# First layer's MLP gate moved from VectorE to TensorE, and the second layer's modulation issued piece by piece, in a two-layer hybrid diffusion backbone

## The chip, the cores and the metric

The kernel runs on one core of a Trainium2 chip. The metric is the device time of one execution in microseconds; the time before is the median of three runs, 2549.3 us (2545.8 to 2554.59). PE below is TensorE, DVE is VectorE, ACT is ScalarE, POOL is GpSimd, and SP is the engine whose queue issues nearly all loads and stores.

## The reference, cut to what matters

Two layers run over 512 latent and 256 context tokens of 1024 features. Each layer makes six vectors of modulation for each of the two streams from a conditioning vector, and uses them as shift, scale and gate around the attention (the first three) and around the MLP (the last three).

```python
mod   = silu(c) @ w_mod[l] + b_mod[l]          # 6 * 1024 values, latent stream
mod_c = silu(c_ctx) @ w_mod[l] + b_mod[l]      # the same, context stream
sh1, sc1, g1, sh2, sc2, g2 = split(mod, 6)     # kinds 0, 1, 2, 3, 4, 5 below
h = modulate(rms_norm(x), sh1, sc1)
...                                            # projections, three attention branches, merge
x = x + g1 * y
x = x + g2 * square(relu(modulate(rms_norm(x), sh2, sc2) @ w_mlp_in)) @ w_mlp_out
```

The second layer updates the latent stream alone. "Kind 5" below is g2, the gate of the MLP.

## The kernel before

The residual is kept transposed: features on the 128 partitions (8 tiles `x[j]`), tokens on the free axis, 768 in the first layer and 512 in the second. Every float32 product is made of three products of rounded parts and remainders (`wh`, `wl` of a weight, `hh`, `hl` of an activation). A weight arrives in pieces of 128x1024 (512 KB): SP loads `wr` (two buffers), ACT rounds it to `wh`, POOL makes the remainder `wl` (`piece`, L197 and L199).

A layer runs as phase 1 (projections; chunk by chunk of 256 columns, products `pb` at L481 to L483, then norms and rotations on DVE, results stored to DRAM), phase 2 (attention with the gate logits `g` between its steps), phase 3 (merge and output projection) and phase 4 (MLP). The MLP runs over eight groups g of 512 hidden features: `up(g + 1)` makes the next group's squared relu (PSUM tile `mi`, `r` and `uh` on ACT, `u` on POOL, `ul` on DVE at L1307) and `down(g)` adds group g into the residual (PSUM tile `mo`; on DVE `x += g2 * mo` at L1261, called resid below, once for 512 and once for 256 tokens of each of 8 feature tiles).

The modulation is made in three ways. (1) `mod_first` makes kinds 0 and 1 of the first layer on PE. (2) `mod_units` makes kinds 2, 4 and 3 of the first layer on PE during its projections: 24 pieces of 128x1024 (tile `wm`, two buffers, loaded by SP at L306), four pieces for a unit of 512 features; after every chunk of the projections two pieces are multiplied (`mod_pe`, L266: 8 small products a piece, 32 columns wide, four of them in the four column groups of the array); after the fourth piece ACT copies the sum out, PE transposes it (L274), and two small DVE steps write `mod` (L314). (3) `mod_step` makes the rest on DVE in the first layer's MLP: one step loads a piece (`wm<-in_wmod`, L249, again two buffers of the name `wm`) and multiplies and sums it over the free axis (L252, called a reduction below), once for each stream that is asked for. 56 steps are queued by `mod_start`: kind 5 of the first layer and kinds 1 and 0 of the second for both streams (24 steps, 48 reductions), and the other four kinds of the second for the latent stream (32 steps, 32 reductions). They are issued eight ahead of `down(0)` and nine after each `down`.

The program is written in the order of these functions; a scheduler then sets the order of each engine's queue from priorities and its own estimate of when things are ready. An engine runs its queue strictly in order, SP too.

Of the kernel before, what the change touches and what calls it, by code (L numbers as in the profile page):

```python
"""Two layers of the hybrid diffusion backbone (MLA + windowed GQA + differential attention).

The residual stream is kept transposed (features on partitions, tokens on the free axis, latent
tokens first, context tokens after them).  Products run in float32r: every float32 operand is split
exactly into a rounded part and a remainder, and the three products that matter at float32
accuracy (hi*hi, lo*hi, hi*lo) are accumulated in PSUM.
"""
# [27 lines left out]
# columns of w_in  # L35
C_QLAT, C_KVLAT, C_KPE, C_SQ, C_SK, C_SV, C_DQ, C_DK, C_DV, C_G = (
    0, 256, 384, 416, 928, 1056, 1184, 1696, 2208, 2720)
# rope order of a head: [first halves of row and column | second halves of row and column]
# [3 lines left out]
# broadcast vectors of a layer  # L42
V_MQ, V_MK, V_SQ, V_SK, V_DQ, V_DK, V_SINK, V_L = 0, 96, 192, 256, 320, 384, 448, 456
NV = 456 + 256
# per-partition vectors of a layer
P_GA, P_GM, P_BM, P_GQ, P_GKV, P_GS = 0, 8, 16, 64, 66, 67
NP_ = 68
# constants
# [30 lines left out]
def _layout(inp):  # L79
    """Host side: permutations and concatenations only."""  # L80
    g = {n: np.asarray(a) for n, a in inp.items()}
    f = lambda a: np.ascontiguousarray(a, dtype=np.float32)
    o = {}
# [3 lines left out]
    # units of four feature blocks: shift and scale of the first norm by pairs of feature tiles, then kinds 2, 4 and 3  # L87
    a = g["w_mod"][0, :, :2048].reshape(KT, 128, 2, 4, 256).transpose(3, 1, 0, 2, 4)
    o["wm0"] = f(a.reshape(4, 128, KT * 512))
    a = g["w_mod"][0].reshape(4, 2, 128, 6, 2, 512)[:, :, :, [2, 4, 3]].transpose(3, 4, 0, 2, 1, 5)  # L90
    o["wm1"] = f(a.reshape(6, 4, 128, 1024))
# [45 lines left out]
class Build:  # L137
    def __init__(self, tc, ins, out):
        self.tc = tc
        self.nc = tc.nc  # L140
        self.ins = ins
        self.out = out
        self.n = 0
        self.mq = []
        self.early = False
        self.gains = {}
        self.F1, self.WD, self.WC = 0.3, 1.5, 0.4   # how the gates are spread over the attention
        self.px = 0

# [11 lines left out]
    def R(self, name, dt=F32):  # L161
        """a [128, 768] tile of the phase's pool"""
# [8 lines left out]
    def psx(self, name):  # L171
        """one bank for a dense product, from both tags in turn"""
# [16 lines left out]
    def piece(self, src, n=1024, own=0):  # L189
        """hi, lo of a piece of weights; own: the number of slots it takes of the phase's pool in place of the common  # L190
        ones."""
# [10 lines left out]
    def mm3(self, out, ah, al, bh, bl, start, stop):  # L202
        """out += (ah + al).T @ (bh + bl) but for al.T @ bl."""
# [9 lines left out]
    def dense_steps(self, ps, w, x, c):  # L213
        """ps = sum of w.T @ x[:, c]; w: [(hi, lo)] stationary [128, 128] blocks, x: [(hi, lo)] moving."""
# [8 lines left out]
    def split_sb(self, src, n=768):  # L223
        """hi, lo of an SBUF tile."""
# [7 lines left out]
    def mod_start(self, kinds):  # L232
        """queue up mod = silu(c) @ w_mod + b_mod for the given sixths, features on partitions."""
# [27 lines left out]
    def mod_pe(self, w, ks, ps):  # L261
        """ps[32 g + stream, 128 features] += 2 silu(c) @ w for four feature blocks g; w [128, len(ks), 512]."""
# [7 lines left out]
    def mod_out(self, ps, pt):  # L270
        """[128 features, 4 blocks, 32]: twice the modulation without its bias."""
# [5 lines left out]
    def mod_first(self, q):  # L277
        """shift and scale of the first norm for feature tiles 2q and 2q + 1, in two steps."""
# [18 lines left out]
    def mod_units(self, n):  # L297
        """n pieces of the modulation of kinds 2, 4 and 3 of the first layer."""
        nc = self.nc
        for _ in range(n):  # L300
            if self.mu == 24:
                return
# [7 lines left out]
            if i == 3:  # L310
                v = self.mod_out(self.mps, self.mps[:, 512:640])
                o = (2, 4, 3)[u // 2] * 8 + u % 2 * 4
# [4 lines left out]
    def first_norm(self, x, h):  # L317
        """the first norm, feature tiles as their modulation arrives, and the query latent of the first layer: PSUM
        tiles [128 tokens, 256]."""
# [45 lines left out]
    def norm_gain(self, l, which, s, k=None):  # L365
        """128 * g * (1 + scale) per feature (rows_rsq gives 1 / 128); of feature tiles k and k + 1 alone at every even k."""
# [19 lines left out]
    def add_square(self, acc, x, j, c, sq, eng):  # L386
        """acc += x_j ** 2 on columns c; sq: a scratch tile."""
# [1142 lines left out]
```

## Time and profile before

| what | value |
|---|---|
| median of three runs | 2549.3 us |
| lowest and highest run | 2545.8, 2554.59 us |
| span of the profiled execution (first to last instruction) | 2547.0 us |
| PE busy, share of the span | 2432.5 us, 96% |
| DVE busy, share of the span | 1537.6 us, 60% |
| first layer's projections | about 84 to 270 us |
| first layer's MLP | about 935 to 1490 us |

The page gives no other time of that execution than its span, which is 2.3 us below the median of the runs. PE is the busy engine throughout; the time that it stands idle is 114.5 us (2547.0 less 2432.5). In the tables of waits, a row names the engine that waited, the tile that it was to write and its line, and behind the arrow what it waited for; then the sum in us, how often, and the longest.

### The profile page before, as it was taken

The numbers are of one execution on the slowest core, as the hardware profiler recorded it, in microseconds if no ns is written. First come the engines' busy times: TensorE is split into PE (matmuls) and PEld (weight loads), VectorE is DVE, ScalarE is ACT, GpSimd is POOL, SyncE is SP. The second block draws the span as 40 slices with busy tenths as digits, with TensorE's granted clock in tenths as the row PEclk, the third lists the DMA queues.
The fourth block names the chain that finished last, engine by engine and source line by source line (L and its number), as shares of the span: only waits on it lengthen the run. The fifth ranks groups of instructions, "written<-read, shape, count | busy, mean of one in ns | idle before, by whom it ended". The sixth has DMA issues, their size and how long they took to land. (4 is left out here: it accounts for less than half of the span.)

```text
span 2547.0 us, 40061 instructions
## 1 busy us (share of the span) xinstructions
PE 2432.5 (96%) x15466; PEld 2136.6 (84%) x15466; DVE 1537.6 (60%) x3081; ACT 1079.7 (42%) x2105; POOL 915.1 (36%) x629
## 2 busy tenths in 40 slices
PE   6999999999999998999999989999999999999999
PEld 5989888888888887888888989998878777888888
DVE  6547777878874479872222277777788874621112
ACT  4343566667652233212222244346666632422321
POOL 2434211111115326434333354441222235454543
PEclk9999999999999999999999999999999999999999
DMA  7265322222346225662111122443323344222222
GB/s 280 90 222 203 131 97 84 96 77 94 100 137 226 94 76 171 214 231 75 59 67 66 60 99 86 173 153 95 103 83 118 110 156 155 83 92 99 91 100 83
DMA packets 133182, 307.38 MB, mean 121 GB/s; under 512 B 43264, under 2 KB 49536, under 8 KB 132608
## 3 DMA queue, kind: packets, MB, share of 16 engines
q1 hardware_dynamic: 122624, 281.23, 32.6%
q10 hardware_dynamic: 10368, 23.60, 2.4%
q8 instruction: 122, 2.00, 0.3%
q14 instruction: 68, 0.56, 0.1%
HBM read 252.08 MB, written 52.70 MB: 120 GB/s over the span
## 5 line engine op out<-in xcount | busy, mean ns | idle before, releaser
L199 POOL TENSOR_TENSOR wl<-wr,wh 128x1024 fp32r<-128x1024 f32 (+2 forms) x266 | 652.6, 2457 | 1139.2 <-ACT wh L197 1066.8
L197 ACT ACTIVATE wh<-wr 128x1024 fp32r<-128x1024 f32 (+2 forms) x266 | 279.5, 1052 | 581.2 <-PE mo L219 317.6
L218 PE MATMUL mo<-uh,wh 128*128 128x512 f32 (+1 forms) x832 | 286.4, 344 | 18.6 <-DVE x L1261 13.6
L219 PE MATMUL mi<-hl,wh 128*128 128x512 f32 (+1 forms) x832 | 285.7, 344 | 3.3 <-DVE hl L434 3.3
L220 PE MATMUL mi<-hh,wl 128*128 128x512 f32 (+1 forms) x832 | 285.2, 343 | 0.0
L218 PE MATMUL mi<-hh,wh 128*128 128x512 f32 (+1 forms) x832 | 284.8, 344 | 0.3 <-DVE x L1261 0.3
L219 PE MATMUL mo<-ul,wh 128*128 128x512 f32 (+1 forms) x832 | 283.8, 341 | 0.0
L220 PE MATMUL mo<-uh,wl 128*128 128x512 f32 (+1 forms) x832 | 283.1, 341 | 0.0
L1307 DVE TENSOR_TENSOR ul<-u,uh 128x512 fp32r<-128x512 f32 (+1 forms) x104 | 80.7, 777 | 304.0 <-POOL u L1306 301.7
L1261 DVE SCALAR_TENSOR_TENSOR x<-mo,mod,x 128x512 f32<-128x512 f32 (+1 forms) x208 | 127.9, 625 | 200.6 <-PE mo L220 200.6
L481 PE MATMUL pb<-wh,hh 128*128 128x256 f32 (+1 forms) x832 | 244.2, 294 | 0.0
L482 PE MATMUL pb<-wl,hh 128*128 128x256 f32 (+1 forms) x832 | 243.2, 292 | 0.8 <-POOL wl L199 0.8
L483 PE MATMUL pb<-wh,hl 128*128 128x256 f32 (+1 forms) x832 | 243.3, 293 | 0.0
L218 PE MATMUL g<-hh,wh 128*128 128x512 f32 (+1 forms) x576 | 212.2, 368 | 0.0
L220 PE MATMUL g<-hh,wl 128*128 128x512 f32 (+1 forms) x576 | 211.8, 368 | 0.0
L219 PE MATMUL g<-hl,wh 128*128 128x512 f32 (+1 forms) x576 | 211.5, 367 | 0.0
L868 ACT ACTIVATE pth<-pT 128x512 fp32r<-128x512 f32 (+3 forms) x344 | 154.1, 462 | 101.7 <-PE pT L865 90.4
L218 PEld LDWEIGHTS mo<-uh,wh 128*128 128x128 f32 x832 | 157.3, 189 | 39.1 <-DVE x L1261 14.9
L869 DVE TENSOR_TENSOR ptl<-pT,pth 128x512 fp32r<-128x512 f32 (+3 forms) x344 | 171.9, 516 | 24.8 <-ACT pth L868 22.6
L219 PEld LDWEIGHTS mi<-hl,wh 128*128 128x128 f32 x832 | 157.3, 189 | 23.5 <-DVE hl L434 3.7
L218 PEld LDWEIGHTS mi<-hh,wh 128*128 128x128 f32 x832 | 156.8, 189 | 20.4 <-DVE x L1261 0.5
L220 PEld LDWEIGHTS mi<-hh,wl 128*128 128x128 f32 x832 | 157.3, 189 | 19.8
(243 smaller groups left out, 5932.5 us busy)
## 6 DMA issues: line engine op xcount, KB each, us to landing
wr<-in_wmi SPq DMA_DIRECT2D x64, 512.0 KB, 3.5
wr<-in_wmo SPq DMA_DIRECT2D x64, 512.0 KB, 3.5
wm<-in_wmod SPq DMA_DIRECT2D x56, 512.0 KB, 3.6
wr<-in_wg SPq DMA_DIRECT2D x48, 512.0 KB, 3.6
wr<-in_wb SPq DMA_DIRECT2D x36, 512.0 KB, 4.2
wm<-in_wm SPq DMA_DIRECT2D x28, 512.0 KB, 4.5
wr<-in_wup SPq DMA_DIRECT2D x24, 512.0 KB, 3.5
gd<-gt ACTq DMA_DIRECT2D x24, 384.0 KB, 2.4
```

What stands on the lines that cost most here:

```text
L197: nc.scalar.activation(out=hi[:, :n], in_=raw[:, :n], func=AF.Copy)
L199: nc.gpsimd.tensor_tensor(out=lo[:, :n], in0=raw[:, :n], in1=hi[:, :n].bitcast(F32), op=ALU.subtract)
L218: mm(ps, lhsT=wh, rhs=xh[:, c], start=i == 0, stop=False)
L219: mm(ps, lhsT=wh, rhs=xl[:, c], start=False, stop=False)
L220: mm(ps, lhsT=wl, rhs=xh[:, c], start=False, stop=i == n - 1)
L481: mm(ps[:, :n], lhsT=ah[:, cs], rhs=wh, start=k == 0, stop=False)
L482: mm(ps[:, :n], lhsT=ah[:, cs], rhs=wl, start=False, stop=False)
L483: mm(ps[:, :n], lhsT=al[:, cs], rhs=wh, start=False, stop=k == nk - 1)
L868: nc.scalar.activation(out=hv[:, k0:k0 + n, qs], in_=pv, func=AF.Copy)
L869: nc.vector.tensor_tensor(out=lv[:, k0:k0 + n, qs], in0=pv, in1=hv[:, k0:k0 + n, qs].bitcast(F32), op=ALU.subtract)
L1261: self.nc.vector.scalar_tensor_tensor(out=x[j][:, c], in0=ps, scalar=g, in1=x[j][:, c], op0=ALU.mult, op1=ALU.add)
L1307: nc.vector.tensor_tensor(out=b[:, c], in0=u, in1=a[:, c].bitcast(F32), op=ALU.subtract)
```

## The change

Kind 5 of the first layer becomes two more units of `mod_units`: 32 pieces in place of 24, three after each of the first four chunks of the projections and two after each of the ten others. `mod_start` no longer queues it, so 48 steps are left (16 for both streams, 32 for the latent one, 64 reductions). They are issued two at a time ahead of each weight piece of `down`, eight per group. The comments go as well, so line numbers above 1300 differ by a few; below that they stay.

```diff
-    a = g["w_mod"][0].reshape(4, 2, 128, 6, 2, 512)[:, :, :, [2, 4, 3]].transpose(3, 4, 0, 2, 1, 5)
-    o["wm1"] = f(a.reshape(6, 4, 128, 1024))
+    a = g["w_mod"][0].reshape(4, 2, 128, 6, 2, 512)[:, :, :, [2, 4, 3, 5]].transpose(3, 4, 0, 2, 1, 5)
+    o["wm1"] = f(a.reshape(8, 4, 128, 1024))
...
     def mod_units(self, n):
         for _ in range(n):
-            if self.mu == 24:
+            if self.mu == 32:
                 return
...
-                o = (2, 4, 3)[u // 2] * 8 + u % 2 * 4
+                o = (2, 4, 3, 5)[u // 2] * 8 + u % 2 * 4
...
             F[f]()
             if l == 0:
-                self.mod_units(2)
+                self.mod_units(3 if self.mu < 12 else 2)
...
             for jp in range(4):
+                self.mod_step(2)
                 hi, lo = self.piece(self.ins["wmo"][l, g, jp])
...
         for g in range(8):
             if g < 7:
                 up(g + 1)
-            if g == 0:
-                self.mod_step(8)
             down(g)
-            self.mod_step(9)
...
-                        self.mod_start([(0, 5, (0, 1)), (1, 1, (0, 1)), (1, 0, (0, 1))]
+                        self.mod_start([(1, 1, (0, 1)), (1, 0, (0, 1))]
                                        + [(1, kd, (0,)) for kd in (2, 4, 3, 5)])
```

What this does to the queues is seen at three places. Names carry the scheduler's numbers; a number is one buffer of a tile.

First, PE after the first chunk of the projections. Before, two pieces (`wm_1178`, `wm_1189`) stand behind that chunk's last products:

```order
L481 MATMUL pb_1116<-wh_981,hh_122 128x256
L482 MATMUL pb_1116<-wl_983,hh_122 128x256
L483 MATMUL pb_1116<-wh_981,hl_123 128x256
L266 MATMUL pm_1180<-wm_1178,sl 32x128 x8
L266 MATMUL pm_1180<-wm_1189,sl 32x128 x8
L481 MATMUL pb_1212<-wh_1201,hh_108 128x256
L482 MATMUL pb_1212<-wl_1203,hh_108 128x256
```

Now the same two stand there, and a third (`wm_1199`) 24 products further on, at the end of the next accumulation:

```order
L483 MATMUL pb_1222<-wh_1217,hl_121 128x256
L481 MATMUL pb_1222<-wh_1217,hh_122 128x256
L482 MATMUL pb_1222<-wl_1219,hh_122 128x256
L483 MATMUL pb_1222<-wh_1217,hl_123 128x256
L266 MATMUL pm_1180<-wm_1199,sl 32x128 x8
L481 MATMUL pb_1248<-wh_1211,hh_108 128x256
L482 MATMUL pb_1248<-wl_1213,hh_108 128x256
```

The third piece has only the buffer of the first one to land in. After the second chunk the third piece stands 24 products behind, after the third chunk 20, and after the fourth two pieces stand 33 rows behind.

Second, SP at the end of the projections, where `ld<-km` loads the keys of the first head of the attention. Before:

```order
L744 DMA qm_2862<-rc_2761 128x192
L744 DMA qm_2865<-rc_2761 128x192
L194 DMA wr_3815<-in_wg 128x1024
L194 DMA wr_4093<-in_wg 128x1024
L790 DMA ld_3122<-km_2166 128x576
L665 DMA qd_3094<-raw_2905 128x768
```

Now:

```order
L744 DMA qm_2908<-rc_2807 128x192
L744 DMA qm_2911<-rc_2807 128x192
L306 DMA wm_3378<-in_wm 128x1024
L306 DMA wm_3388<-in_wm 128x1024
L194 DMA wr_3907<-in_wg 128x1024
L194 DMA wr_4185<-in_wg 128x1024
L790 DMA ld_3189<-km_2212 128x576
L665 DMA qd_3140<-raw_2951 128x768
```

The last two pieces of the modulation stand ahead of the weights of the gate logits and of the keys. On PE the transposes of these keys (L780) stood behind three accumulations `pb` and five products `g`; they now stand behind the first pair of the last unit and three accumulations, and the last pair, its transpose and the five products follow them.

Third, DVE in the first layer's MLP, around the first resid. Before (`x_10233` is feature tile 0; each L252 row that writes a `dump` is one reduction):

```order
L258 TENSOR_TENSOR mod_73<-modr_75,vp_72 128x8
L258 TENSOR_TENSOR mod_74<-modr_76,vp_72 128x8
L1307 TENSOR_TENSOR ul_11685<-u_11718,uh_11684 128x256
L252 ISA dump_12098,modr_75<-wm_12096,silu_10978 128x1024
L252 ISA modr_75 128x1
L1261 SCALAR_TENSOR_TENSOR x_10233<-mo_11804,mod_68,x_10233 128x512
L1261 SCALAR_TENSOR_TENSOR x_10233<-mo_11818,mod_69,x_10233 128x256
L252 ISA dump_12100,modr_76<-wm_12096,silu_10980 128x1024
```

Now:

```order
L258 TENSOR_TENSOR mod_73<-modr_75,vp_72 128x8
L258 TENSOR_TENSOR mod_74<-modr_76,vp_72 128x8
L1307 TENSOR_TENSOR ul_11777<-u_11810,uh_11776 128x256
L252 ISA dump_12998,modr_75<-wm_12996,silu_11070 128x1024
L252 ISA modr_75 128x1
L1261 SCALAR_TENSOR_TENSOR x_10325<-mo_11858,mod_68,x_10325 128x512
L1261 SCALAR_TENSOR_TENSOR x_10325<-mo_11872,mod_69,x_10325 128x256
L252 ISA dump_13002,modr_75<-wm_13000,silu_11070 128x1024
```

From the first reduction to this resid the queue holds 33 reductions and 14 `ul` steps before, and 33 and 14 now; the reductions are other ones (before, the first 16 are kind 5 of the first layer). Between the first and the sixteenth resid, that is through `down(0)`, it holds 14 before and 10 now; between `down(0)` and `down(1)` 14 and 14; through `down(1)` 12 and 7; after it 7 and none.

## Rows read from the trace of the kernel before

**Rows 1.** The page, busy time of each engine over the span.

```profile
PE 2432.5 (96%) x15466; PEld 2136.6 (84%) x15466; DVE 1537.6 (60%) x3081; ACT 1079.7 (42%) x2105; POOL 915.1 (36%) x629
```

**Rows 2.** Waits of PE, whole span: waited for, us in total, times, longest.

```profile
PE tp L780 <- DMA ld<-km: 4.0, 1, 4.0
...
PE pm L266 <- DMA wm<-in_wm: 2.7, 2, 2.4
```

**Rows 3.** Waits of PE, 940 to 1160 us (first layer's MLP, first groups).

```profile
PE mo L218 <- DVE x L1261: 12.1, 4, 8.0
PE mo L218 <- ACT r L1304: 3.5, 1, 3.5
```

**Rows 4.** Timeline of PE in `down(0)`: start, us, what, idle before it.

```profile
1011.82 0.58 PE L218 MATMUL mo<-uh,wh 128*128 128x256 f32 x1 [3.50 <-ACT r L1304]
...
1022.79 0.79 PE L218 MATMUL mo<-uh,wh 128*128 128x512 f32 x1 [8.05 <-DVE x L1261]
```

**Rows 5.** Windows: length, PE, PEld, DVE, ACT, POOL busy, granted clock, DMA, GB/s.

```profile
1024.00:1028.00 4.00, 4.00 (x11) 3.11 (x10) 3.97 (x13) 0.00 (x0) 0.00 (x0) 0.50 0.68 236
1028.00:1032.00 4.00, 4.00 (x24) 3.51 (x23) 3.82 (x7) 1.06 (x1) 1.13 (x1) 0.95 0.48 158
```

**Rows 6.** Timeline of DVE: first reduction, end of kind 5, first resid.

```profile
949.94 1.56 DVE L252 CUSTOM_DVE_ANT_0 dump<-wm,silu 128x1024 bf16<-128x1024 f32 x1 [1.52 <-DMA wm<-in_wmod]
...
986.87 2.42 DVE L258 TENSOR_TENSOR mod<-modr,vp 128x8 f32<-128x8 f32 x2
...
1021.99 1.14 DVE L1261 SCALAR_TENSOR_TENSOR x<-mo,mod,x 128x512 f32<-128x512 f32 x2
```

**Rows 7.** Window of line L252 alone: length, DVE busy, granted clock, DMA, GB/s.

```profile
945.00:1022.00 77.00, 55.71 (x66) 0.95 0.52 173
```

**Rows 8.** The same window, line L1307 (`ul`) alone.

```profile
945.00:1022.00 77.00, 16.27 (x18) 0.95 0.52 173
```

**Rows 9.** Timeline of DVE in `down(1)`: a reduction and the resid behind it.

```profile
1110.49 2.54 DVE L252 CUSTOM_DVE_ANT_0 dump<-wm,silu 128x1024 bf16<-128x1024 f32 x1 [1.33 <-DMA wm<-in_wmod]
1112.95 0.74 DVE L1261 SCALAR_TENSOR_TENSOR x<-mo,mod,x 128x512 f32<-128x512 f32 x1
```

**Rows 10.** Timeline of PE: two pieces of modulation, then a transpose, between products.

```profile
128.65 0.28 PE L483 MATMUL pb<-wh,hl 128*128 128x256 f32 x1
128.86 1.08 PE L266 MATMUL pm<-wm,sl 128*32 128x128 f32 x32
129.87 0.38 PE L481 MATMUL pb<-wh,hh 128*128 128x256 f32 x1
...
131.51 0.28 PE L482 MATMUL pb<-wl,hh 128*128 128x256 f32 x1
131.68 0.33 PE L274 MATMUL pm<-kc,me 128*128 128x128 f32 x1
...
131.96 0.28 PE L481 MATMUL pb<-wh,hh 128*128 128x256 f32 x1
```

**Rows 11.** SP's queue: the next two pieces, issued behind that pair.

```profile
129.56 0.81 SPq L306 DMA_DIRECT2D wm<-in_wm  x2
```

**Rows 12.** Line L306, all 24 pieces: time from issue to landing.

```profile
DMA to landing us min/median/max: 3.4/4.4/7.5
```

**Rows 13.** SP's queue at the end of the projections.

```profile
264.28 0.88 SPq L194 DMA_DIRECT2D wr<-in_wg  x2
265.25 0.38 SPq L790 DMA_DIRECT2D ld<-km  x1
```

**Rows 14.** Timeline of PE at the same place.

```profile
265.33 0.39 PE L218 MATMUL g<-hh,wh 128*128 128x512 f32 x1
...
270.68 0.85 PE L780 MATMUL tp<-identr,ld 128*96 128x128 f32 x6 [4.03 <-DMA ld<-km]
```

**Rows 15.** Window inside that wait, columns as in rows 5.

```profile
267.00:268.00 1.00, 0.00 (x0) 0.00 (x0) 1.00 (x5) 0.00 (x0) 0.00 (x0) 1.00 1.09 381
```

**Rows 16.** Timeline of DVE: its last idle time before 270 us.

```profile
233.48 1.75 DVE L463 TENSOR_REDUCE ss<-sqs 128x24 f32<-128x1536 f32 x1 [3.47 <-ACT sqs L462]
```

## The prediction

> **What bounds the kernel now.** The page comes first: PE is busy for 96% of the span, DVE for 60% [rows 1]. So what counts is work added to PE and time for which PE stands still. The table of PE's waits then says where the two places of this change lie. In the first layer's MLP, PE waits 12.1 us in four goes for a resid of DVE (DVE adds a `mo` into the residual and so frees PSUM), and 3.5 us for an ACT step [rows 3]. In the projections it waits 2.7 us for pieces of modulation and 4.0 us for the keys of the first head [rows 2].
>
> The timeline of PE shows that most of the MLP's waits are one cluster at the start of `down(0)`: 3.50 us before 1011.82, and 8.05 us before 1022.79 [rows 4]. Behind it the granted clock is 0.50, the 1.2 GHz level, until about 1028.3: the window from 1024 to 1028 holds 11 products, the next one 24 at clock 0.95 [rows 5]. From 1022.8 to 1028.3 that is 5.5 us at half speed, 2.75 us lost. The cluster costs some 14 us.
>
> Why is the resid late? Kind 5, the gate that it needs, was complete at 986.87 + 2.42 = 989.3 us [rows 6], yet the first resid starts at 1021.99 [rows 6], 33 us later. It doesn't wait for the gate. It stands in DVE's queue behind 33 reductions and 14 `ul` steps: of 77 us, the reductions take 55.71 us (66 records, two for each) [rows 7] and the `ul` steps some 16 us [rows 8], nearly all of it.
>
> **The change in the MLP.** In the new order 33 reductions and 14 `ul` steps again stand ahead of the first resid. The 16 reductions of kind 5 are gone from the program, but later ones have moved up into their places. Since the dependency on the gate ended no wait here, and the queue did, I leave the cluster as it is: 0 us, with the four small steps that prepare the next norm's gain, which now stand ahead of the resid, as its only difference. DVE's total falls by 16 x 55.71 / 33 = 27 us, but almost all of that falls where DVE doesn't hold PE up.
>
> What can be gained is behind the cluster: 12.1 - 8.05 = 4.05 us in three waits during `down(1)` [rows 3, 4]. They arise where a reduction waits for its own load and a resid is queued behind it (idle 1.33 us for the DMA, reduction 2.54 us, resid after it) [rows 9]. `down(1)` now holds 7 reductions among its 16 resids in place of 12, all in its first half, but `down(0)` now gets ten that each need their own load, where two used to share one. I take half, -2.0 us; the bounds are -4.05 (all three go) and +2 (`down(0)` gets half as much of this as `down(1)` had, and `down(1)` loses nothing).
>
> **The change in the projections: the work.** Two pieces cost PE 129.87 - 128.65 = 1.22 us between two products that otherwise start 0.12 us apart, so 1.1 us a pair, and a transpose (131.96 - 131.51) less two such steps, 0.2 us [rows 10]. Eight pieces and two transposes come to 4.4 + 0.4 = 4.8 us. ACT's two copies and DVE's four steps of 0.15 us are small beside what these engines have free. The loads, 8 x 512 KB, are only moved from the MLP.
>
> A page speaks against this price. These products are in full float32, and the Trainium skill, "FP8 and Floating Point Precision", TensorE Precision Notes, says true FP32 takes four passes through the array; with "TensorE: Matmul & The Clock Gate", section "Wait — 56ns, not 53.3ns?", at 56 ns for 128 columns, 64 products would make an estimated 64 x 4 x 56 ns = 14.3 us and raise the sum by about 10 us. The rows deny it: 16 such products take 1.1 us here, 69 ns each, so they overlap, and I keep 4.4 us.
>
> **The projections: the waits.** With two buffers a third piece can be loaded only when the first has been used. SP issues such a load 129.56 - 128.86 = 0.70 us after a pair starts [rows 10, 11] and it lands 3.4 us later at best, 4.4 in the median [rows 12]: at 4.1 or 5.1 us. PE is there after 1.1 us and 24 products of 0.12 us, at 4.0 us; behind the third chunk after 20 products, at 3.5 us. So the third pieces of the first three chunks wait 0.1 + 0.1 + 0.6 = 0.8 us at best, and 1.1 + 1.1 + 1.6 = 3.8 us with median landings. I take 2.5 us. The two pieces behind the fourth chunk stand 33 rows back, and I add nothing; the upper bound has a wait like today's 2.4 us [rows 2] more.
>
> Nothing downstream absorbs this. DVE's last idle time before 270 us ended at 233.48 with a step that waited for ACT's square of a fresh projection [rows 16], so it follows PE; from there DVE works without a gap, and its last results are what SP stores ahead of `ld<-km`. By then four of the eight pieces and one transpose have been added: 2.2 + 0.2 + 2.5 = 4.9 us later.
>
> **The projections: the end.** SP issues two loads of gate weights at 264.28 and `ld<-km` at 265.25; it lands at about 270.7, and PE, which would be free at 266.65, waits 4.03 us for it [rows 13, 14]. Now two more loads of 512 KB stand ahead in the same queue. At the 381 GB/s that the DMA engines moved there [rows 15] 1.05 MB takes 2.75 us. The bounds are 0 (these are hidden) and 4.4, a whole landing [rows 12]. I take 2.75, since the queue was the only one at work in that window.
>
> Of what else moves, the first pair of the last unit lies ahead of that wait and is hidden by it: PE is then ready some 2 us after its old time plus the delay of 4.9 us less the products below, well before the keys. If this cover were gone it would cost 1.1 us. Behind the wait come the last pair and its transpose, 1.3 us, and the five products of the gates that used to run before it, from 265.33 to 266.65 [rows 14], 1.3 us: 2.6 us. The longer wait also costs clock, by rows 5 up to 2.75 us for 8 us of standing still; the present wait already costs part of it, so 0.5 us, with 0 and 1.5 as ends.
>
> **The sum.** Projections: 2.4 (four pieces, a transpose) + 2.5 (third pieces) + 2.75 (keys) + 2.6 (behind the wait) + 0.5 (clock) = +10.75 us. MLP: -2.0 us. Net +8.8 us on the span of 2547.0, so 2555.8. The span lies 2.3 us below the median of the runs, 2549.3; carried over, 2558.1 us. The bounds: at least 2.4 + 0.8 + 0 + 2.6 + 0 - 4.05 = +1.8, at most 2.4 + 6.2 + 4.4 + 2.6 + 1.5 + 2 = +19.
>
> **Rivals.**
> (1) The waits are absorbed: third pieces land in time and the two loads ahead of the keys cost nothing, so little more than PE's own work is added. That is 2.4 + 0.8 + 2.6 - 2.0 = +3.8, some 2553. For it: the DMA engines have gaps in the first chunks, and the best landing of 3.4 us nearly suffices. Against it: the median landing doesn't, and the keys are behind 1 MB more in one queue. It decides if the third pieces wait under 1 us and the keys come no more than 5 us later than now.
> (2) The change does what it says: the first resid is free of the modulation, and the cluster goes. Then 3.50 + 8.05 + 2.75 = 14.3 us come back in place of 0: 8.8 - 14.3 = -5.5, some 2544, and with rival 1 on top -10.5, some 2539. For it: the 14 us are really there, and DVE has 27 us less to do. Against it: the order on DVE, 33 and 33. It would take reductions that run 8 us faster in sum over the same stretch.
> (3) Loads get in each other's way in the projections: each third piece waits with a median landing (3.8 us) and the fourth chunk 2.4 us more, the keys a whole landing: 2.4 + 6.2 + 4.4 + 2.6 + 1.5 - 2.0 = +15.1, some 2564.
>
> **How the numbers follow.** Chances: my forecast 0.45, rival (1) 0.29, rival (2) 0.12, rival (3) 0.14. A difference under 0.3%, 7.6 us, is about what a measurement of this kernel can tell from no change. My forecast lies just above that; I count 0.75 of its chance as slower. Slower: 0.45 x 0.75 + 0.14 = 0.48. Faster: rival (2) reaches beyond -7.6 us only along with rival (1), but may gain more in `down(1)`, so two thirds of it, 0.08. The rest, 0.44, is within 0.3%. The range from 2548 to 2565 takes in the forecast and rivals (1) and (3), 0.88 less their outer edges, and leaves out rival (2); its low end is that of the bound, +1.8, less some scatter of the runs (2545.8 to 2554.59).
>
> **What would show it.** In the profile after: the 3.5 and 8 us waits stand again at the start of `down(0)`, with the clock at 0.50 behind them, and the first resid is queued behind 33 reductions; if they are gone, the central step is wrong. PE's wait for `wm<-in_wm` grows from 2.7 to about 5 us. The wait for `ld<-km` grows from 4.0 to about 7 us, and the first scores come some 10 us later than now. The waits for L1261 behind the cluster fall from 4.05 to about 2 us. If the projections end less than 5 us later, the waits were mis-sized and rival (1) holds.

## The result, and the profile after

The changed kernel takes 2567.0 us (median of four runs, 2562.39 to 2568.93) against 2549.3 us for the kernel before. The ratio is 1.0064, with a 95% interval of 1.0045 to 1.0082: 0.0064 x 2549.3 = 16.3 us slower, 11.5 to 20.9. The forecast was 2558, from 2548 to 2565. It had the direction and half of the size.

The page after, answering [rows 1]: PE has 11.6 us more to do, of which the added products are a part, and DVE has 19.6 us less, where 27 were forecast.

```profile
PE 2444.1 (95%) x15596; PEld 2146.4 (84%) x15596; DVE 1518.0 (59%) x3051; ACT 1080.4 (42%) x2107; POOL 910.3 (35%) x629
```

Waits of PE in the projections, 60 to 320 us (waited for, us in total, times, longest), answering [rows 2]. The keys took 4.0 us and the pieces 2.7; now 6.7 and 5.3:

```profile
PE tp L780 <- DMA ld<-km: 6.7, 1, 6.7
PE pm L266 <- DMA wm<-in_wm: 5.3, 5, 2.7
```

Waits of PE in the first layer's MLP, 960 to 1180 us, answering [rows 3]: 12.1 us have become 13.6, and the 3.5 us stand as they were.

```profile
PE mo L218 <- DVE x L1261: 13.6, 4, 8.1
PE mo L218 <- ACT r L1304: 3.5, 1, 3.5
```

The timeline of PE shows the cluster of [rows 4] again, and behind it the waits in `down(1)`, the first of which was 1.17 us before:

```profile
1032.19 0.56 PE L218 MATMUL mo<-uh,wh 128*128 128x256 f32 x1 [3.52 <-ACT r L1304]
1043.17 0.79 PE L218 MATMUL mo<-uh,wh 128*128 128x512 f32 x1 [8.07 <-DVE x L1261]
...
1115.66 0.50 PE L218 MATMUL mo<-uh,wh 128*128 128x512 f32 x1 [2.58 <-DVE x L1261]
1126.23 0.51 PE L218 MATMUL mo<-uh,wh 128*128 128x512 f32 x1 [1.68 <-DVE x L1261]
1136.15 0.50 PE L218 MATMUL mo<-uh,wh 128*128 128x512 f32 x1 [1.30 <-DVE x L1261]
```

The granted clock behind the 8.07 us is 0.50 as in [rows 5], and the reductions ahead of the first resid fill as much of DVE as in [rows 7] (window of line L252 alone, then the first resid itself):

```profile
1044.00:1048.00 4.00, 4.00 (x10) 3.06 (x10) 3.45 (x7) 0.00 (x0) 0.00 (x0) 0.50 0.65 232
...
966.00:1042.00 76.00, 55.07 (x65) 0.96 0.52 174
...
1042.37 1.14 DVE L1261 SCALAR_TENSOR_TENSOR x<-mo,mod,x 128x512 f32<-128x512 f32 x2
```

**Where the time went.** In the table, the same products of PE are looked up in each trace, and the entry is how much later (in us) they start than in the trace of before. The columns are the time of that product before: the first transposes of the first `lora` (98), a product `g` early in the attention (333), one in its middle (579), the first product of the MLP (915), of `down(0)` (997), one behind `down(1)` (1152), one in the second layer (1591), and the end of the span. The other kernels are explained below.

```
kernel                              98     333     579     915     997    1152    1591     end
changed                           -0.2   +14.1   +17.4   +18.5   +20.0   +22.4   +22.9   +20.1
1  gate on PE alone               -0.9   +10.8   +10.4   +11.7   +13.2   +18.0   +17.4   +16.9
2  third buffer                   -0.3    +6.5    +6.7    +8.0    +9.5   +14.3   +14.1    +9.4
3  third buffer, early            -1.7    +3.0    +2.9    +4.2    +5.7    +8.8    +8.0   +12.4
4  changed, reductions held       -1.6   +13.7   +13.1   +14.5   +16.9    -3.6    -4.6    -7.6
5  products alone                 -0.2    -0.4    -0.9    +2.0    +3.4    +6.3    +6.4    +7.4
6  loads alone                    -0.1   +14.1   +14.7   +17.1   +18.5   +18.0   +18.6   +19.6
7  gate left out                  -2.1    -2.4    -2.6    -1.4    +0.1    +4.8    +4.3    +0.3
8  before, reductions held        -2.1    -2.7    -2.9    -1.7    -0.2   -20.8   -21.0   -27.3
9  third pieces spread            -2.0   +12.0   +12.1   +12.9   +12.9   +17.0   +16.5   +23.0
10 early and held                 -2.1    +1.3    +1.1    +3.7    +6.0   -14.5   -14.8   -14.5
```

A difference of two columns is what a stage costs. Projections (98 to 333): 14.3 us in the changed kernel, 11.7 in kernel 1, whose queues are the same. PE's window over that stage (columns as in rows 5), before, then after, splits this: PE stands still for 13.4 us in place of 7.5, and it is busy for 8.5 us more.

```profile
98.32:333.07 234.75, 227.21 (x1985) 211.78 (x1985) 153.58 (x351) 104.24 (x206) 78.71 (x55) 0.98 0.50 173
...
98.12:347.21 249.09, 235.74 (x2115) 217.37 (x2115) 158.17 (x355) 104.86 (x208) 77.25 (x55) 0.97 0.52 180
```

Beginning of the MLP (997 to 1152): +2.4 and +4.8. Two parts of the 20.1 us don't belong to the change. Between 333 and 579, 3.3 us come from one load that landed late in this execution (last section); kernel 1 doesn't have them. Between 579 and 997 every kernel loses to that one execution of before, whatever was edited: 0.8 to 4.9 us, most of them about 3, kernels 7 and 8 with unchanged projections too.

### The profile page after: what moved, and what is told of

Its sections match the earlier page's. It is cut to its first block, busy times and chain, and to the rows that moved or that the text cites. A ratio compares the mean times of both kernels' runs of the same rounds, so it can differ in the third digit from the quotient of the medians.

```text
span 2567.1 us, 40292 instructions
## 1 busy us (share of the span) xinstructions
PE 2444.1 (95%) x15596; PEld 2146.4 (84%) x15596; DVE 1518.0 (59%) x3051; ACT 1080.4 (42%) x2107; POOL 910.3 (35%) x629
## 5 line engine op out<-in xcount | busy, mean ns | idle before, releaser
L1307 DVE TENSOR_TENSOR ul<-u,uh 128x512 fp32r<-128x512 f32 (+1 forms) x104 | 76.8, 739 | 332.7 <-POOL u L1306 325.9
```

Of the source, the lines that this page charges most:

```text
L1307: nc.vector.tensor_tensor(out=b[:, c], in0=u, in1=a[:, c].bitcast(F32), op=ALU.subtract)
```

## The experiments

The theory after the result: what is lost is lost in the projections, by the added loads first of all, and the MLP loses a little too instead of gaining. The rivals were that the issue of two steps per weight piece costs something, that the products are the cost, or that the MLP did gain and something else ate it. Times are medians; a ratio is to runs of the kernel before that were made along with it, with its 95% interval. Before took 2553.9 us (20 runs) for kernels 1 to 4, 2552.9 (25 runs) for 5 to 8, 2547.8 (7 runs) for 9 and 10.

```
kernel                          median us   ratio    interval
1  gate on PE alone               2565.6    1.0053   1.0037 to 1.0069
2  third buffer                   2560.0    1.0035   1.0017 to 1.0052
3  third buffer, early            2558.4    1.0017   0.9998 to 1.0037
4  changed, reductions held       2541.1    0.9950   0.9934 to 0.9966
5  products alone                 2559.7    1.0018   1.0000 to 1.0037
6  loads alone                    2564.8    1.0040   1.0023 to 1.0057
7  gate left out                  2555.1    1.0001   0.9982 to 1.0021
8  before, reductions held        2524.9    0.9881   0.9843 to 0.9919
9  third pieces spread            2571.6    1.0093   1.0075 to 1.0111
10 early and held                 2534.1    0.9939   0.9915 to 0.9963
```

**1. The gate on PE alone.** The changed kernel, with the steps issued where they were before:

```diff
             for jp in range(4):
-                self.mod_step(2)
                 hi, lo = self.piece(self.ins["wmo"][l, g, jp])
...
+            if g == 0:
+                self.mod_step(8)
             down(g)
+            self.mod_step(9)
```

> The first half of the change alone: kind 5 on PE in the projections, the other 48 steps issued as before (eight ahead of down(0), nine after each down). The scheduler puts every engine's queue in the same order as in the changed kernel. Theory (all of the loss comes from the projections and what follows from them; issuing two per weight piece does nothing): 2567 us, within 4 us of the changed kernel, the cluster of 3.5 and 8.1 us at down(0) again. Rival (the new issue places cost something in the MLP): about 2.5 us less, 2564, with the waits behind the cluster back at 4.1 us in place of 5.6.

1.0053 against 1.0064, one within the interval of the other. The scheduler brings both programs to the same order on all five queues, row for row, so the second half of the change does nothing, and kernel 1 is the changed kernel run again. The cluster stands (3.50 and 8.61 us); the waits behind it are not back at 4.1 us but at 6.1. The rival falls. What differs between the two profiles, 14.3 and 11.7 us in the projections and 2.4 and 4.8 in the MLP, is scatter, and single stages below are no surer than that.

**2 and 3. A third buffer, and early pieces.**

```diff
-                with self.phase("p1", ND=5, NPB=3, NM=2):
+                with self.phase("p1", ND=5, NPB=3, NM=3):
```

and for kernel 3 also

```diff
-                self.mod_units(3 if self.mu < 12 else 2)
+                self.mod_units(3 if self.mu < 18 else 2)
```

> The changed kernel with three buffers instead of two for the pieces of modulation in the projections, so that a third piece needn't wait for the first to be used; one load stands ahead of the keys in SP's queue in place of two. Theory (waits for third pieces, and the half clock behind the longest of them, make some 5 to 7 us of the loss): PE's wait for the pieces falls from 5.3 to under 1 us, no granted clock of 0.50 at 220 us, DVE's chain to the keys 4 to 6 us earlier, 2560 us. Rival (the added products and loads cost what they cost, and waits only move): under 2 us less, 2565 us or more.

> As the kernel with three buffers, with three pieces after each of the first six chunks, so that all 32 are multiplied before the keys are transposed and no load of them stands ahead of the keys in SP's queue. Theory (the two loads ahead of the keys are worth 1.5 to 2.7 us on top): the wait for the keys goes from 6.7 back to 4 or 5 us, 2557 us; what then remains over the kernel before is the work of the 64 products, about 5 us, and 2 us in the MLP. Rival (the keys wait for DMA bandwidth, whatever stands ahead): the wait stays at 6 us or more and the time at that of the kernel with three buffers alone.

Waits of PE in the projections, kernel 2, then kernel 3:

```profile
PE tp L780 <- DVE raw L468: 6.0, 1, 6.0
...
PE pm L266 <- DMA wm<-in_wm: 1.6, 2, 1.4
```

```profile
PE tp L780 <- DMA ld<-km: 4.6, 1, 4.6
...
PE pm L266 <- DMA wm<-in_wm: 1.5, 2, 0.9
```

The waits for pieces go to about 1.5 us, and the projections lose 6.8 and 4.7 us in place of 14.3 and 11.7. In kernel 2 the wait of 6.0 us is the one ahead of the keys' transposes, though the page puts it down to a step of DVE; in kernel 3, without loads ahead of them, the keys are waited for 4.6 us, nearly as before (4.0). What is left in kernel 3 is PE's own work, as was expected: PE stands still for 8.5 us over the projections (7.5 before) and is busy for 3.9 more (231.1 in place of 227.2). As a whole kernel 2 lies at +8.9 us (0.0035 x 2553.9) and kernel 3 at +4.3, its interval just reaching no change; the intervals of kernels 1, 2 and 3 touch, so that the order of the three rests on the stage. The profile of kernel 3 holds a wait of 6.2 us of another origin, in the second layer (last section).

**4. The reductions held.** The changed kernel, with every reduction queued on DVE behind the resid that precedes it in the program:

```diff
             for jp in range(4):
-                self.mod_step(2)
+                if g or jp:
+                    with self.tc.issue_after(self.lr.ins):
+                        self.mod_step(2)
...
-        self.nc.vector.scalar_tensor_tensor(out=x[j][:, c], in0=ps, scalar=g,
+        self.lr = self.nc.vector.scalar_tensor_tensor(out=x[j][:, c], in0=ps, scalar=g,
```

> The changed kernel with every reduction held on DVE behind the resid that precedes it in the program, so that none stands ahead of the first resid (33 in the changed kernel) and at most four between two resids. Theory (the cluster at down(0) is DVE's queue, not the gate): the waits of 3.5 and 8.1 us and the half clock behind them go, and most of the 5.6 us behind; 14 to 20 us less than the changed kernel, 2547 to 2553 us. Rival (PE waits for something else there, such as ACT's relu or the weights): the waits stay under another name, 2563 us or more.

The cluster is gone, with the waits behind it; what PE still waits for between 940 and 1180 us lies ahead of `down(0)`, in the norm and the first `up`:

```profile
PE st L402 <- DVE acc L393: 1.6, 1, 1.6
PE mi L218 <- DVE x L1261: 0.3, 1, 0.3
```

On DVE the first resid now follows the last `ul` directly, and the reductions come behind it:

```profile
1018.16 0.42 DVE L1307 TENSOR_TENSOR ul<-u,uh 128x256 fp32r<-128x256 f32 x1 [4.37 <-POOL u L1306]
1018.51 1.14 DVE L1261 SCALAR_TENSOR_TENSOR x<-mo,mod,x 128x512 f32<-128x512 f32 x2
...
1022.88 1.22 DVE L252 CUSTOM_DVE_ANT_0 dump<-wm,silu 128x1024 bf16<-128x1024 f32 x1
```

From 997 to 1152 the table has -20.5 us, against +2.4 in the changed kernel: 22.9 us between them. The queue theory holds, and the queue cost more than was expected: 2541.1 us came in place of 2547 to 2553. The 3.5 us that the profile puts down to ACT's `r` went too, so they were the same queue seen one step earlier.

**5 and 6. The products alone and the loads alone,** each added to the kernel before. Kernel 5 multiplies the piece that was loaded last (`self.lw`) and drops the result; kernel 6 loads eight more pieces and reads each with one product of the usual eight:

```diff
+            w = self.lw
+            self.mod_pe(w, (2 * i, 2 * i + 1), self.eps)
```

```diff
+            w = self.ph.tile([128, 1024], F32, tag="wm", bufs=self.NM, name=self.nm("wm"))
+            nc.sync.dma_start(w, self.ins["wm1"][self.me // 5, i])
...
+            self.nc.tensor.matmul(self.eps[0:32, 0:128], lhsT=self.sl[:, i, :], rhs=w[:, 0:128], start=i == 0, stop=i == 3,
+                                  tile_position=(0, 0))
```

> The kernel before, with the added work of PE alone: 64 more products and two transposes in the projections, one piece's worth after each of the first four chunks and two after each of the last two. They multiply the piece that was loaded last, so there is no added load, and their sum goes to a tile that nothing uses. Theory (what costs most is the loads: third pieces that come late and the keys behind two loads): the work shows at its price of 4.8 us, no wait for pieces beyond today's 2.7, the wait for the keys no longer than 4.0: +5 us to the kernel before. Rival (the products cost more than their price, by the clock or by the delay of DVE's chain): +9 us or more.

> The kernel before, with the added loads alone: eight more pieces of 512 KB in the two buffers of the projections, one after each of the first four chunks and two after each of the last two, each read by one product of the usual eight, so that it holds its buffer. The result is unused. Theory (the loads are what costs): third pieces wait 2.5 to 5 us, the keys behind two loads 1.5 to 2.7 us longer, and clock on top: +6 to +9 us. Rival (the loads are hidden and the products are the cost): +2 us or less.

Products: +4.6 us (0.0018 x 2552.9; 0 to 9.4) for the whole kernel, and -0.2 us in the projections. Loads: +10.2 us (5.9 to 14.6) for the whole, and +14.2 us in the projections. Expected were +5 and +6 to +9. The waits there, products alone first (no wait for the keys is left in it), then loads alone (`pe` is the added sum):

```profile
PE pm L266 <- DMA wm<-in_wm: 1.4, 3, 0.8
```

```profile
PE pm L266 <- DMA wm<-in_wm: 6.1, 3, 2.7
PE pe L307 <- DMA wm<-in_wm: 4.2, 4, 2.5
...
PE tp L799 <- DMA ld<-km: 2.5, 1, 2.5
```

The -0.2 us doesn't show that the products are free. The scheduler changed the order of SP and PE around the keys as well: in kernel 5 the keys are issued at 262.35 us in place of 265.25 [rows 13], and the wait of 4.0 us for them is gone. SP's issue, the window of PE over the projections (before: above) and the window of tile `pe` alone:

```profile
262.35 0.38 SPq L807 DMA_DIRECT2D ld<-km  x1
...
98.17:332.67 234.50, 230.28 (x2115) 213.61 (x2115) 152.97 (x355) 105.26 (x208) 79.66 (x55) 0.99 0.51 173
...
98.00:348.00 250.00, 5.58 (x130) 3.86 (x130) 0.53 (x4) 0.56 (x2) 0.99 0.50 169
```

The added products and transposes take 5.6 us. PE is busy for 3.1 us more than before, the granted clock being a little higher, and it stands still for 3.3 less (4.2 in place of 7.5), so that the stage comes out even.

Kernel 6 isn't free of products either: the products that read them take 3.0 us of PE (tile `pe`). Its wait for the keys is shorter and not longer, as was expected, because two waits for pieces (2.55 and 0.91 us, at 277.27 and 278.58) stand right ahead of it; the three make 6.0 us, near the 6.7 of the changed kernel.

So the loads bring the waits, and are the larger part of the loss; the products bring their price, which a lucky order can hide. The whole kernels say the same: 4.6 + 10.2 = 14.8 us, within the 11.5 to 20.9 of the changed kernel. How the loss of the stage splits exactly is not settled by one execution each.

**7. The gate left out.** Before, without kind 5 in the MLP:

```diff
-                        self.mod_start([(0, 5, (0, 1)), (1, 1, (0, 1)), (1, 0, (0, 1))]
+                        self.mod_start([(1, 1, (0, 1)), (1, 0, (0, 1))]
...
+        for s in (0, 1):
+            nc.vector.tensor_copy(self.mod[0][s][:, 40:48], self.vp[0][:, P_BM + 40:P_BM + 48])
```

> The kernel before, with kind 5 of the first layer left out: its 8 steps (16 reductions, 8 loads) are gone from the MLP and the gate is set to its bias, so the first layer's gate is not that of the reference. The projections stay as before, and the MLP's queues on PE, DVE and ACT are those of the changed kernel. The prediction's step for the MLP said -2.0 us. Theory now (the cluster stands with 33 reductions ahead, and the waits behind it grow from 4.1 to 5.6 us): +1 to +4 us to the kernel before, although 16 reductions are gone. Rival (the MLP really gets faster by the prediction's step, and what the changed kernel lost there came from other places): -2 us.

The whole kernel is at 1.0001, from 0.9982 to 1.0021: too wide to tell +1 to +4 us from -2. The stage says more: +4.6 us from 997 to 1152. The six profiles with the changed order of the MLP have 2.4, 4.8, 4.8, 3.1, 4.7 and 4.1 us there (the changed kernel and kernels 1, 2, 3, 7 and 9), 4.0 in the mean; the three with the order of before have 0, 2.9 and -0.5 (before and kernels 5 and 6), 0.8 in the mean. The two groups overlap, by 2.4 and 2.9. What tells them apart better is PE's first wait in `down(1)`: 2.58 to 2.80 us in all six, 1.17, 2.36 and 1.24 us in the three; and in five of the six half clock follows it, in none of the three. The window behind that wait, before, then kernel 7:

```profile
1094.00:1098.00 4.00, 4.00 (x24) 3.48 (x25) 3.14 (x6) 0.00 (x0) 0.00 (x0) 1.00 0.70 236
...
1097.00:1101.00 4.00, 4.00 (x13) 3.13 (x13) 1.94 (x4) 0.00 (x0) 0.00 (x0) 0.57 0.89 301
```

At 0.57 for 4 us, 0.43 x 4 = 1.7 us are lost. With sixteen reductions fewer the MLP gets some 3 us slower in the mean, about half of it by waits and half by the clock. The -2 us are nowhere to be seen.

**8. The kernel before, with its later reductions held.** Kind 5 stays ahead of `down(0)`; the other 48 steps are issued as in kernel 4.

```diff
             if g == 0:
                 self.mod_step(8)
             down(g)
-            self.mod_step(9)
...
             for jp in range(4):
+                if g or jp:
+                    with self.tc.issue_after(self.lr.ins):
+                        self.mod_step(2)
```

> The kernel before, with the 16 reductions of kind 5 ahead of the first resid as they are, and every later one held on DVE behind the resid that precedes it in the program: 16 in place of 33 ahead of the first resid, at most four between two resids. Theory (the gate itself was never late, only DVE's queue): the cluster goes here as well, without moving the gate to PE, and the time falls by some 18 to 22 us, as the held version of the changed kernel fell by 24 to 26: about 2531 us, below every other version. Rival (16 reductions and the loads that they wait for still hold the first resid): 2543 us or more.

2524.9 us, 0.9881 of the kernel before (0.9843 to 0.9919): the fastest of all, 42 us below the changed kernel (28 us below the runs of before made along with it, and below the 2531 expected). The stage from 997 to 1152 loses 20.6 us, as in kernels 4 and 10 (20.5 each), so the 16 reductions that still stand ahead of the first resid cost nothing there. Of the other 7 us, 6.3 come behind 1591, where kernels 2 and 7 gain 4.7 and 4.0 without that edit; whether they are its doing is not shown. All 80 reductions are still made on DVE, and not one product has been added to PE.

**9. The third pieces spread.**

```diff
-                self.mod_units(3 if self.mu < 12 else 2)
+                self.mod_units(3 if self.mu in (6, 11, 16, 21) else 2)
```

> The changed kernel with the four third pieces after the 4th, 6th, 8th and 10th chunk of the projections in place of the first four; two buffers, the same loads and products, the same two loads ahead of the keys. Theory (a third piece waits wherever two buffers are used up, and the longest wait, 2.7 us behind the fourth chunk with half clock after it, is not special to that place): PE's wait for pieces stays at 4 to 6 us and the time at 2565 us, within 4 us of the changed kernel. Rival (the fourth chunk was a bad place: its two pieces and the clock behind them made 4 to 5 us): 2561 us, with under 2 us of waits for pieces.

```profile
PE tp L780 <- DMA ld<-km: 6.8, 1, 6.8
PE pm L266 <- DMA wm<-in_wm: 5.1, 6, 2.3
```

5.1 us of waits for pieces and 14.0 us in the projections, as in the changed kernel: the first four chunks are not a bad place by themselves, and in both places that were tried two buffers are too few for a third piece. The time, 2571.6 us, is above what was expected; some 6.5 us of it came in the second layer (last section).

**10. Early and held:** kernels 3 and 4 together.

> The gate on PE as in the changed kernel, with both remedies: three buffers and three pieces after each of the first six chunks, and every reduction held behind the resid that precedes it. Theory (the two losses are independent): the 25 us of the held version and the 8 us of the version with three buffers add up, 2567 - 25 - 8 = 2534 us; that is some 9 us above the kernel before with its reductions held (2525 us), because the 64 products on PE are paid and the 16 reductions that they replace were hidden on DVE. Rival (once the cluster is gone, DVE's work ahead of the first resid counts, and 16 fewer reductions pay for the products): 2525 us or less.

2534.1 us, as expected; the two losses add up. It lies 9 us above kernel 8, and by the ratios 0.0058 x 2550 = 15 us. The two intervals just meet (0.9915 and 0.9919), so that even with both remedies the gate on PE is probably, not surely, a loss. Of the 12.8 us between the two profiles, the projections make 4.0 (+3.4 here, -0.6 in kernel 8), as the products' price would; 2.2 come between 579 and 997, and 6.6 behind 1591, where kernel 8 has the 6.3 named above. These are not settled.

## Why the prediction was wrong, point by point

**The central step was right.** That the first resid waits for DVE's queue and not for its gate, and that 33 reductions ahead of it before and after leave the cluster where it is, is what the profile shows (3.52 and 8.07 us, clock 0.50) and what kernels 4 and 8 show by taking the queue away. Rival (2) fell as argued. But the cluster was priced too low. I counted 3.50 + 8.05 + 2.75 us = 14.3; the queue costs about 20.5 us (kernel 8). The 4.05 us of the three waits behind it belong to the same queue, and half clock follows the first wait too, which I hadn't counted: the 12 products between the two waits, 2.9 us, run at 0.50, 1.5 us lost (before, window 1011.8 to 1014.7).

**The MLP step failed in its sign.** I took -2.0 us, because `down(1)` holds 7 reductions in place of 12. The stage became about 3 us slower (kernel 7 and the means above). I counted how many reductions stand among the resids. The two later waits of `down(1)` stayed as they were (1.72 and 1.18 us before, 1.68 and 1.30 now), with 7 reductions as with 12, and the first one, for the first resid, grew from 1.17 to 2.58. DVE ahead of that resid, in the changed kernel:

```profile
1109.97 1.23 DVE L252 CUSTOM_DVE_ANT_0 dump<-wm,silu 128x1024 bf16<-128x1024 f32 x1 [1.37 <-DMA wm<-in_wmod]
...
1111.23 2.23 DVE L258 TENSOR_TENSOR mod<-modr,vp 128x8 f32<-128x8 f32 x1
1113.39 1.21 DVE L252 CUSTOM_DVE_ANT_0 dump<-wm,silu 128x1024 bf16<-128x1024 f32 x1
...
1114.53 0.41 DVE L1307 TENSOR_TENSOR ul<-u,uh 128x256 fp32r<-128x256 f32 x1
1114.87 0.74 DVE L1261 SCALAR_TENSOR_TENSOR x<-mo,mod,x 128x512 f32<-128x512 f32 x1
```

A reduction that waited for its load, the small addition that ends a kind (2.23 us here), one more reduction and an `ul` stand in the way; before, that addition lay 16 us ahead of the resid, at 1077.16. That this makes the wait grow is a guess that was not tried apart, and kernel 5 speaks against it as the whole cause: with DVE's order of before it waited 2.36 us at the same place. The cause of the grown wait stays open. The sign cost some 5 of the 9 us by which the forecast missed.

**The projections were 1 to 4 us too cheap.** 10.75 us were forecast, of which 0.5 for clock; 14.3 and 11.7 came. By their terms:

- Waits for pieces: 2.5 us more were forecast, 2.6 came (2.7 to 5.3). It fits partly by luck. The third pieces of the first three chunks waited 0.22 + 0.15 + 1.94 = 2.3 us and today's wait of 2.45 us went, which I had not counted; the two pieces behind the fourth chunk, for which I added nothing, waited 0.32 and 2.69 us. The long wait has no fixed place: in kernel 1, the same program, the third chunk's piece waited 2.87 us and these two 0.45 and 0.27.
- The clock behind that last wait was missing. The timeline of PE and the window behind it (columns as in rows 5):

```profile
219.18 0.65 PE L266 MATMUL pm<-wm,sl 128*32 128x128 f32 x16 [2.69 <-DMA wm<-in_wm]
...
219.00:223.00 4.00, 3.82 (x31) 3.62 (x32) 1.82 (x5) 1.33 (x2) 1.44 (x1) 0.61 0.55 180
```

  At 0.61 for 4 us, 0.39 x 4 = 1.6 us are lost. In kernel 1 the half clock follows its own long wait (0.50 from 182 to 185 us).
- So DVE's chain to the keys came later than the 4.9 us that I had. Its last idle time ended at 233.48 before and ends at 241.36 now, 7.9 us later:

```profile
241.36 1.75 DVE L463 TENSOR_REDUCE ss<-sqs 128x24 f32<-128x1536 f32 x1 [4.35 <-ACT sqs L462]
```

- The keys: 2.75 us longer forecast, 6.66 - 4.03 = 2.63 us came. SP issues the two loads, the two of gate weights and then the keys:

```profile
272.17 0.87 SPq L306 DMA_DIRECT2D wm<-in_wm  x2
273.13 0.86 SPq L194 DMA_DIRECT2D wr<-in_wg  x2
274.03 0.59 SPq L790 DMA_DIRECT2D ld<-km  x1
...
280.98 0.84 PE L780 MATMUL tp<-identr,ld 128*96 128x128 f32 x6 [6.66 <-DMA ld<-km]
281.75 1.94 PE L266 MATMUL pm<-wm,sl 128*32 128x128 f32 x32
```

- Behind the wait: 2.6 us forecast, 14.1 - 10.3 = 3.8 came (10.3 is 280.98 - 270.68). The last pair runs at half clock and takes 1.94 us where [rows 10] has 1.08.

**What was mis-sized.** Taken together, the waits came as forecast: 2.5 + 2.75 = 5.25 us were forecast, and PE stands still for 5.8 us more (4.8 in kernel 1). What was too small is PE's busy time in the stage: it grew by 8.5 us (6.9 in kernel 1), where 4.8 were priced for all products and transposes, 1.1 of them hidden, and 0.5 for clock. The pieces and transposes (tile `pm`) take 22.69 us in place of 16.15, 6.5 more, part of that at half clock; the same work takes 5.6 us in kernel 5 and 5.0 in kernel 3 (21.18). Of the rest, 2.0 us, half clock is a part: 0.61 from 219 to 223 us, and again behind the keys. The loads, of which I had written that they "are only moved from the MLP", bring the waits and the clock behind them, so more of the loss than the products do; kernel 3, with three buffers and no load ahead of the keys, gets 7.0 to 9.6 of the 11.7 to 14.3 us back.

Rival (1) would have needed third pieces that wait under 1 us. Rival (3) came nearest in time, 2564, with the longest wait behind the fourth chunk, for which only it and my upper bound had a price; but it had the gain of 2.0 us in the MLP as well, so its number is near partly by luck.

**The range** ended at 2565, 2 us short. It took the outer bound of +19 as too unlikely; the MLP's own bound was +2, where about +3 came, so the bound was too narrow as well.

## What to carry to other kernels

Work that is moved off an engine for the sake of a late instruction helps only if it stood ahead of that instruction in the queue and nothing moves up into its place: look at the new order. Here holding the reductions behind the resid gains 28 us, 20.6 of them in the stage that it is meant for, and the move of the gate to another engine loses 16. And when work moves, its loads move: price them against the buffers and the queue of the place that they go to, and the clock behind each wait, as well as the arithmetic.

## What the runs showed of the hardware

**The same wait costs clock in one execution and not in another.** The wait ahead of the norm in the last output tile is 3.40 us in both traces (PE's timeline, before, then after), and the stretches of 3 us behind it have the clock at 1.00 with 27 products, and at 0.58 with 14:

```profile
924.46 0.70 PE L416 MATMUL nr<-dg,kc 128*128 128x256 f32 x2 [3.40 <-DVE dg L405]
...
925.00:928.00 3.00, 3.00 (x27) 3.00 (x25) 2.54 (x6) 1.34 (x4) 0.00 (x0) 1.00 0.31 124
```

```profile
942.98 0.75 PE L416 MATMUL nr<-dg,kc 128*128 128x256 f32 x2 [3.40 <-DVE dg L405]
...
943.00:946.00 3.00, 3.00 (x14) 2.95 (x15) 2.05 (x5) 0.91 (x2) 0.00 (x0) 0.58 0.43 165
```

Over the 4 us from 943 us the clock is 0.57, so 0.43 x 4 = 1.7 us are lost, and all the later kernels but kernel 9 lost that much there against this one execution of before. It makes single stages uncertain by as much. Shorter waits do the same, now and then: 2.59 us in `down(1)` of kernel 3 were followed by 0.60 over 4 us, the 2.58 us there in the changed kernel by 1.00. So did 2.04 us, at 428.16 in the changed kernel, where a load of values landed 2 us later than before (6.1 us behind its issue in place of 4.1) with the DMA engines almost idle (share 0.01 from 426 to 428):

```profile
428.16 0.69 PE L865 MATMUL pT<-kc,p 128*128 128x128 f32 x2 [2.04 <-DVE ptl L869]
...
428.00:431.00 3.00, 2.84 (x10) 2.46 (x11) 1.98 (x6) 1.84 (x7) 1.46 (x2) 0.51 0.00 0
```

**Small DVE steps can take 13 times as long beside POOL.** In kernels 3 and 9, whose queues in the second layer have the same order as the changed kernel's, a weight's remainder on POOL fell on the chain of small DVE steps that ends in the keys. POOL's two remainders, and the DVE steps beside them, in kernel 9:

```profile
1703.52 4.76 POOL L199 TENSOR_TENSOR wl<-wr,wh 128x1024 fp32r<-128x1024 f32 x2 [3.22 <-ACT wh L197]
```

```profile
1703.44 0.18 DVE L453 SCALAR_TENSOR_TENSOR a<-a,v 128x16 f32<-128x16 f32 x1
1703.65 2.31 DVE L454 SCALAR_TENSOR_TENSOR y<-a,y 128x16 f32<-128x16 f32 x1
1705.99 2.32 DVE L452 TENSOR_TENSOR a<-y 128x16 f32<-128x16 f32 x1
1708.35 0.17 DVE L453 SCALAR_TENSOR_TENSOR a<-a,v 128x16 f32<-128x16 f32 x1
...
1716.18 0.84 PE L780 MATMUL tp<-identr,ld 128*96 128x128 f32 x6 [6.78 <-DMA ld<-km]
```

Steps of 0.17 us took 2.31 and 2.32 us, PE waited 6.78 us for the keys behind them (6.20 in kernel 3), and in the ten other traces that wait is 0.25 us or none. The Trainium skill, "SBUF — State Buffer", section "Who interferes with whom", says that a DVE instruction with two inputs in SBUF contends with a GpSimd instruction that reads SBUF, over a port pair that the two share as an exclusive lock. The trace agrees: 2.3 us is about one remainder on POOL (4.76 us for two). The reductions show it too: in the changed kernel the 17 that met no POOL instruction took 1.22 us each, the 47 others 1.21 to 3.43 us, 1.78 in the mean.
